# Two slots, one product and one dependency moved in the mixer of a two-layer decoder trunk

## The chip, the cores and the metric

The kernel runs on one core of a Trainium2 chip. The core has engines that run side by side, each with its own list of instructions in a fixed order: PE (TensorE) multiplies matrices and transposes, PEld is its loading of weights, DVE (VectorE) and ACT (ScalarE) do elementwise work, POOL (GpSimd) a few small operations, and SP issues the DMA transfers. The metric is the time of one execution in microseconds (us) on the device; smaller is better. Times of single instructions come from one profiled execution.

## The reference

The input x is 256 tokens by 1024 channels in float32. Two layers follow each other, each with a SwiGLU feed-forward (FFN 1), a mixer and a second SwiGLU feed-forward (FFN 2), all three with a residual and a layer norm:

```python
for l in range(DEPTH):
    x = layer_norm(ALPHA * x + 0.5 * swiglu(x, ffn1_gate[l], ffn1_up[l], ffn1_down[l]), ln_g[l, 0], ln_b[l, 0])
    h = x @ w_in[l]
    ...
    y_pool = multiscale_pool(u, pool_w[l], pool_scale[l])
    o = hgrn2_recurrence(q.astype(f32), f_raw.astype(f32), v.astype(f32), lb_all[l])
    y_hgrn = head_rms_norm(o, hgrn_norm_g[l]) * jax.nn.silu(g.astype(f32))
    mix = jnp.concatenate([y_pool.astype(x.dtype), y_hgrn.astype(x.dtype)], axis=-1) @ w_out[l]
    x = layer_norm(ALPHA * x + mix, ln_g[l, 1], ln_b[l, 1])
    x = layer_norm(ALPHA * x + 0.5 * swiglu(x, ffn2_gate[l], ffn2_up[l], ffn2_down[l]), ln_g[l, 2], ln_b[l, 2])
```

The recurrence has four heads of 128 channels. Per head it is causal linear attention with a decay per channel: with b the running sum of log f, the score of query t on key s is the sum over d of q[t,d] k[s,d] exp(b[t,d] - b[s,d]) for s up to t, k = (1 - lb) sigmoid(-f_raw), and the output is scores times v. The matrices x @ W are 1024 wide on the contracted side; the hidden width of the FFN is 2816.

## The kernel before, in words

The 256 tokens are two halves (`hf` 0 and 1) of 128 partitions. Every float32 product of a weight matrix is three matmuls on rounded operands: high by high, high by low, low by high (`mm3`, L96 to L98). The high part is a cast on ACT (L102), the low part the difference on DVE (L103); names with `h` and `l` at the end are such pairs (`wh`, `wl` for the weights of the gates and projections, `dh`, `dl` for the down projection, `xt` for x transposed, `hth`, `htl` for the hidden values). A weight comes as a tile of 512 KB into one of five `raw` buffers; it is cast and split, which frees the raw buffer for the next load.

The FFN takes its hidden width in 11 groups. For the first two groups, `G` (L300 and L96 to L98) makes gate and up for a half into one PSUM tile, `gate` applies the silu on ACT (L333) and the product `hn` on DVE (L334), `T` transposes hn on PE (L406), and `D` is the down projection into `acc`. After the last group comes `layer_norm`: a residual sum (L243), statistics (L244, L245), the root on POOL, then two operations per half row on DVE (L250, L251). The normed x is transposed in two parts of four 128x128 transposes each (L177).

The mixer projects onto five blocks: f, q, v, g and u. From f it makes the key `kn` by a chain of DVE and ACT operations (`post_f`, tiles tA, tB, tC); `flip` (L574) transposes kn and the query, four transposes each, into kT and qT. `decays` builds exponentials EA and EB for a head (L634 on PE, L635 on ACT), multiplies them with kT and qT on DVE (L640, L652) and, for one strip, copies on POOL (L664). `grams` computes the scores of a pair of heads with small matmuls (L681, L686) and selects them into `Pm` under masks (L698, L700). `diagonal` writes the score of a token with itself into Pm. `cross` makes the scores between the halves, `output` the products with v (L722).

What sets the order: PE's list is written by hand, in the order in which the Python code issues it. A counter of slots advances by one with each `mm3`, three 128x512 matmuls; `later(n, f)` runs `f` n slots on, so that small pieces of work fall between the matmuls of a projection. Functions queued for the same slot run in the order in which they were queued. The lists of the other engines are set when the program is built, by priorities and by when a result is expected; `high_priority` (gates, hidden values) moves work ahead and a negative offset (loads, casts and splits of weights) moves it back. Each engine then takes its list strictly in order and waits at an instruction whose operand is not there.

The parts that the change touches:

Of the kernel before, what the change touches and what calls it, by code (L numbers as in the profile page):

```python
# [14 lines left out]
ALU = mybir.AluOpType  # L15
PSUM = bass.MemoryType.PSUM

P = 128
# [56 lines left out]
def trunk(ctx: ExitStack, tc: tile.TileContext, t, out: bass.AP):  # L75
# [153 lines left out]
    def load_gb(l, i):  # L229
# [3 lines left out]
        late_dma(b, t["ln_b"][l, i:i + 1, :].to_broadcast([P, D]))  # L233
        return g, b

    def layer_norm(hf, accs, scale, gb, slots, last=False):
        z = xp.tile([P, D], F32, name="x")
        st = sp.tile([P, 2, 6], F32, name="st")
        mv = sp.tile([P, 2], F32, name="mv")
        rs = sp.tile([P, 1], F32, name="rs")  # L240
        for c in range(2):
            cs = slice(c * 512, c * 512 + 512)
            nc.vector.scalar_tensor_tensor(z[:, cs], accs[c], scale, x[hf][:, cs], ALU.mult, ALU.add)  # L243
            nc.vector.bn_stats(st[:, c, :], z[:, cs])  # L244
        nc.vector.bn_aggr(mv, st.rearrange("p a b -> p (a b)"))  # L245
        nc.vector.tensor_scalar_add(rs, mv[:, 1:2], LN_EPS / ALPHA ** 2)
        nc.gpsimd.tensor_tensor(rs, rs, neghalf[:, 0:1], ALU.pow)
        for c in range(2):
            cs = slice(c * 512, c * 512 + 512)
            nc.vector.scalar_tensor_tensor(z[:, cs], z[:, cs], mv[:, 0:1], gb[0][:, cs], ALU.subtract, ALU.mult)  # L250
            nc.vector.scalar_tensor_tensor(z[:, cs], z[:, cs], rs, gb[1][:, cs], ALU.mult, ALU.add)  # L251
            if last:
                nc.sync.dma_start(out[hf * P:(hf + 1) * P, cs], z[:, cs])
        x[hf] = z
        pinned[0] = PINNED
        if not last:
            xT[hf] = Transposed(hf, z, slots)


    class FFN:  # L260
        def __init__(self, l, w, ln_i, first=False, last=False):
            gu, dn = t["gu"][l, w], t["dn"][l, w]
            self.first, self.last, self.mixer_next = first, last, not w
            self.slots = ((16, 18), (16, 18) if w else (13, 14))
            self.accs = [None, None]
            self.gw, self.dw, self.ht = {}, {}, {}
            self.ln = (l, ln_i)
            self.gb = None
            for g in range(NG):
                self.gw[g] = []  # L270
                for kq in range(4):
                    extra = (4 * g + kq) % (NW + NX) >= NW
                    self.gw[g].append(Weight(gu[g, kq], *(("x", NX) if extra else ("w", NW)), first and g == 0))
                for n in {0: [], 1: [0, 1], 2: [], NG - 1: [NG - 2, NG - 1]}.get(g, [g - 1]):
                    self.dw[n] = [Weight(dn[2 * n + i], "d", ND) for i in range(2)]
# [53 lines left out]
        def gate(self, g, hf, ps):  # L329
            sil = scope[0].tile([P, GW], F32, name="sil", bufs=2)  # L330
            hn = scope[0].tile([P, GW], F32, name="hn", bufs=2)
            with tc.high_priority(offset=AHEAD):
                nc.scalar.activation(sil, ps[:, 0:GW], AF.Silu)  # L333
                nc.vector.tensor_tensor(hn, sil, ps[:, GW:2 * GW], ALU.mult)  # L334

            slots = {(NG - 1, 0): 2, (NG - 1, 1): 4, (1, 1): 4}
            later(slots.get((g, hf), 6), lambda: self.T(g, hf, hn))

        def start(self):
# [179 lines left out]
    def mixer(l, win, wout):  # L519
# [22 lines left out]
        def post_f(hf, ps):  # L542
            f = mp.tile([P, 512], F32, name="tA", bufs=2)
            nc.scalar.copy(f, ps)
            tmp = mp.tile([P, 512], F32, name="tB", bufs=2)
            ls = mp.tile([P, 512], F32, name="tC", bufs=2)
            log_sigmoid(ls, f, tmp)
            if l > 0:
                nc.vector.tensor_tensor(ls, ls, lm, ALU.add)
            kn[hf] = mp.tile([P, 512], F32, name="kn")  # L550
            nc.vector.tensor_tensor(f, ls, f, ALU.subtract)
            nc.scalar.activation(kn[hf], f, AF.Exp)
            if l > 0:
                nc.vector.tensor_tensor(tmp, ls, la, ALU.subtract)
                nc.vector.tensor_tensor(ls, ls, la, ALU.max)
                nc.scalar.activation(tmp, tmp, AF.Abs)
                nc.scalar.activation(tmp, tmp, AF.Exp, scale=-1.0)
                nc.scalar.activation(tmp, tmp, AF.Ln, bias=1.0)
                nc.vector.tensor_tensor(ls, ls, tmp, ALU.add)

            lf[hf] = [mp.tile([P, 512], F32R, name=n, bufs=2) for n in ("la", "lb")]
            first, second = slice(0, 64), slice(64, P)
            for part, here, there in zip(lf[hf], (first, second), (second, first)):
                nc.scalar.copy(part[here], ls[here])
                nc.vector.tensor_tensor(part[there], ls[here], part[here].bitcast(F32), ALU.subtract)

            def go():
                kT[hf] = flip(kn[hf], "kT")
            later(13, go)

        def flip(nat, name):
            pt = psg.tile([P, NH * P], F32, name="gu").rearrange("p (k t) -> p k t", k=NH)
# [6 lines left out]
        def post_q(hf, ps):  # L579
            A256[hf] = mp.tile([P, NH, P], F32, name=f"A{hf}")  # L580
            q = mp.tile([P, 512], F32, name="tA", bufs=2)
            nc.scalar.activation(q, ps, AF.Copy, scale=float(P) ** -0.5)
            def go():
                qT[hf] = flip(q, "qT")
                later(5, lambda: diagonal(hf, q))
                lag = 7 + 4 * l
                for h in range(NH):
                    later(lag + 2 * h, lambda h=h: decays(hf, h))
                later(lag + 9, lambda: grams(hf, 0))
                later(lag + 14, lambda: grams(hf, 1))  # L590
                if hf == 1:
                    later(lag + 17, cross)
            later(4, go)

        def diagonal(hf, q):
# [3 lines left out]
            nc.vector.tensor_tensor(flat, q, kn[hf], ALU.mult)  # L599
            nc.vector.tensor_reduce(dg, prod, mybir.AxisListType.X, ALU.add)  # L600
            Pm[hf] = mp.tile([P, NH, P], F32, name="Pm", bufs=2)
            for h in range(NH):
                nc.vector.tensor_scalar_mul(Pm[hf][:, h, :], ident, dg[:, h:h + 1])

# [17 lines left out]
        def decays(hf, h):  # L624
# [19 lines left out]
            both = halved(EA[:, :, 0:512])  # L644

            side = (k, q)[hf]
            near, other = (1, 0) if hf == 0 else (0, 1)
            ts = [slice(0, 64), slice(64, P)]
            mul(far[:, :, ts[near]], both[:, :, near, fars:fars + 64], side[:, :, ts[near]])
            whole = c1[:, :, top + 63:top + 64] if hf == 0 else c0[:, :, fars + 63:fars + 64]  # L650
            for i in range(2):
                nc.vector.scalar_tensor_tensor(far[:, i, ts[other]], both[:, i, other, fars:fars + 64], whole[:, i, :],  # L652
                                               side[:, i, ts[other]], ALU.mult, ALU.mult)

            mul(halved(EA[:, :, 512:640]), both[:, :, :, top + 128:top + 192], halved(k))
            low, up = halved(k)[:, :, :, 0:32], halved(q)[:, :, :, 32:64]
# [146 lines left out]
        for hf in range(2):  # L803
# [12 lines left out]
                wout[kt].used()  # L816
            if hf == 0:
                place.reverse()
            layer_norm(hf, accs, 1.0 / ALPHA, gb, (15, 17) if hf else (13, 15))
        return guard  # L820

    phases = []
# [85 lines left out]
```

## Time and profile before

| what | us |
|---|---|
| median of 3 runs | 958.29 (958.11 to 958.52) |
| the profiled execution | 958.23 |
| its span, first to last instruction | 956.5 |
| PE busy / DVE busy / ACT busy | 946.6 / 654.8 / 519.6 |
| granted PE clock, share of full speed | 1.0 |

The span is the time from the first to the last instruction of the profiled execution; 1.7 us lie around it. Busy shares are averages over all stages. The timelines below give start and length in us from the span's start; where a row has a bracket, it is the idle time of the engine ahead of it and the instruction that ended it. The next instruction of an engine can start before the last one has ended, so the distance of two starts is what an instruction costs the engine in a dense stretch.

### The profile page before, as it was taken

How to read it: one execution, taken by the hardware profiler on the slowest of the kernel's cores; microseconds unless marked ns; L12 is line 12 of the kernel's file. 1: busy time of each engine (PE TensorE's matmuls, PEld its weight loads, DVE VectorE, ACT ScalarE, POOL GpSimd, SP SyncE). 2: the span in 40 equal slices, each digit the busy share in tenths (PEclk: the TensorE clock that was granted, in tenths of full speed). 3: DMA queues.
4: the chain of work that ended last, by engine and by line, in shares of the span. 5: the costliest groups of instructions: out<-in, count | busy, mean ns of one | idle time of the engine just before them, and what ended most of it. 6: DMA issues, size and time to landing. Idle time of an engine off the chain costs nothing. (4 is left out here: it accounts for less than half of the span.)

```text
span 956.5 us, 13129 instructions
## 1 busy us (share of the span) xinstructions
PE 946.6 (99%) x4817; PEld 800.0 (84%) x4817; DVE 654.8 (68%) x1104; ACT 519.6 (54%) x809; POOL 32.4 (3%) x50
## 2 busy tenths in 40 slices
PE   9999999999999999999999999999999999999996
PEld 7888888888887888888888888888888888888885
DVE  6875656679789765656676565557898896575625
ACT  6765454368456755444445645433985466546420
POOL 0000000001110000000000000000021000000000
PEclk9999999999999999999999999999999999999999
DMA  8977775332627876565346766552327377676301
GB/s 318 336 243 251 254 247 169 109 103 97 219 88 247 311 232 222 191 205 169 123 157 239 237 211 211 174 155 99 110 67 265 112 266 262 222 240 215 114 1 45
DMA packets 50801, 180.22 MB, mean 188 GB/s; under 512 B 6192, under 2 KB 6192, under 8 KB 50736
## 3 DMA queue, kind: packets, MB, share of 16 engines
q1 hardware_dynamic: 50544, 178.85, 55.5%
q8 instruction: 38, 0.62, 0.3%
q0 software_dynamic: 192, 0.53, 0.2%
q14 instruction: 27, 0.22, 0.1%
HBM read 178.30 MB, written 1.05 MB: 188 GB/s over the span
## 5 line engine op out<-in xcount | busy, mean ns | idle before, releaser
L102 ACT CAST wh<-raw 128x1024 fp32r<-128x1024 f32 x196 | 205.1, 1051 | 100.9 <-DMA raw<-in_gu 35.7
L103 DVE TENSOR_TENSOR wl<-raw,wh 128x1024 fp32r<-128x1024 f32 x196 | 235.9, 1219 | 27.0 <-PE gu L300 15.3
L300 PE MATMUL gu<-xt,wh 128*128 128x512 f32 x768 | 180.6, 391 | 0.0
L103 DVE TENSOR_TENSOR dl<-raw,dh 128x1024 fp32r<-128x1024 f32 x88 | 106.5, 1223 | 101.6 <-ACT dh L102 96.0
L300 PEld LDWEIGHTS gu<-xt,wh 128*128 128x128 f32 x768 | 144.1, 188 | 31.7
L102 ACT CAST dh<-raw 128x1024 fp32r<-128x1024 f32 x88 | 91.6, 1049 | 109.7 <-DMA raw<-in_dn 101.3
L96 PE MATMUL acc<-dh,hth 128*128 128x512 f32 x352 | 140.0, 398 | 0.1
L98 PE MATMUL acc<-dh,htl 128*128 128x512 f32 x352 | 138.1, 392 | 0.0
L97 PE MATMUL acc<-dl,hth 128*128 128x512 f32 x352 | 137.4, 390 | 0.0
L96 PE MATMUL gu<-wh,xt 128*128 128x512 f32 x320 | 128.7, 402 | 0.0
L98 PE MATMUL gu<-wh,xt 128*128 128x512 f32 x320 | 125.5, 392 | 0.0
L97 PE MATMUL gu<-wl,xt 128*128 128x512 f32 x320 | 125.0, 391 | 0.0
L300 PE MATMUL gu<-xt,wl 128*128 128x256 f32 x768 | 99.6, 282 | 0.0
L300 PEld LDWEIGHTS gu<-xt,wl 128*128 128x128 f32 x768 | 96.8, 191 | 1.9
L323 DVE TENSOR_TENSOR sil<-gu,sil 128x256 f32<-128x256 f32 x64 | 27.0, 422 | 83.7 <-ACT sil L322 83.7
L98 PEld LDWEIGHTS acc<-dh,htl 128*128 128x128 f32 x352 | 66.0, 188 | 14.8 <-DVE htl L103 0.2
L97 PEld LDWEIGHTS acc<-dl,hth 128*128 128x128 f32 x352 | 66.2, 188 | 12.7 <-DVE dl L103 0.3
L96 PEld LDWEIGHTS acc<-dh,hth 128*128 128x128 f32 x352 | 66.2, 188 | 12.5 <-ACT hth L102 0.5
L98 PEld LDWEIGHTS gu<-wh,xt 128*128 128x128 f32 x320 | 60.1, 188 | 13.1
L97 PEld LDWEIGHTS gu<-wl,xt 128*128 128x128 f32 x320 | 60.2, 188 | 11.4
L96 PEld LDWEIGHTS gu<-wh,xt 128*128 128x128 f32 x320 | 60.1, 188 | 11.0
L300 PE MATMUL gu<-xt,xh 128*128 128x512 f32 x256 | 62.4, 396 | 0.0
(182 smaller groups left out, 1056.2 us busy)
## 6 DMA issues: line engine op xcount, KB each, us to landing
raw<-in_gu SPq DMA_DIRECT2D x172, 512.0 KB, 4.4
raw<-in_dn SPq DMA_DIRECT2D x88, 512.0 KB, 4.6
raw<-in_win SPq DMA_DIRECT2D x40, 512.0 KB, 4.2
raw<-in_wout SPq DMA_DIRECT2D x16, 512.0 KB, 4.2
lng<-in_ln_g SPq DMA_DIRECT2D x6, 512.0 KB, 4.7
lnb<-in_ln_b SPq DMA_DIRECT2D x6, 512.0 KB, 6.0
raw<-in_first SPq DMA_DIRECT2D x5, 384.0 KB, 5.7
x<-in_first SPq DMA_DIRECT2D x3, 384.0 KB, 7.2
```

What stands on the lines that cost most here:

```text
L96: nc.tensor.matmul(ps, lh, wh, start=start, stop=False)
L97: nc.tensor.matmul(ps, lh, wl, start=False, stop=False)
L98: nc.tensor.matmul(ps, ll, wh, start=False, stop=stop)
L102: first = nc.scalar.copy(dst_h, src)
L103: return first, nc.vector.tensor_tensor(dst_l, src, dst_h.bitcast(F32), ALU.subtract)
L300: nc.tensor.matmul(ps[i][part][:, 2 * S - w:], weight.parts[lo][:, c:c + P], x[:, 0:w], start=kt == 0 and not lo, stop=kt == KT - 1 and lo ...
L323: nc.vector.tensor_tensor(dst, p[:, 0:S], dst, ALU.add)
```

## The change

`layer_norm` remembers its last addition. The product hn of the first group and first half, in every FFN but the first, may only be scheduled behind it. The two parts of x's transposes, which had slots of their own, share the earlier slot; in the first FFN the transposes of hn for group 1 of both halves come at slot 5. In the mixer the flip of kn comes at slot 12 after `post_f` in place of 13, the first scores at `lag + 10` in place of 9, and the cross product at `lag + 14`, right behind the second scores of the second half. The diagonal is one product of two broadcast operands in place of four operations. The "far" products, three operations per head pair before, are two: one over the whole tile and one more over a half of it.

```diff
+    normed = [None]
...
-            nc.vector.scalar_tensor_tensor(z[:, cs], z[:, cs], rs, gb[1][:, cs], ALU.mult, ALU.add)
+            normed[0] = nc.vector.scalar_tensor_tensor(z[:, cs], z[:, cs], rs, gb[1][:, cs], ALU.mult, ALU.add)
...
-            self.slots = ((16, 18), (16, 18) if w else (13, 14))
+            self.slots = ((16, 16), (16, 16) if w else (13, 13))
...
-                nc.vector.tensor_tensor(hn, sil, ps[:, GW:2 * GW], ALU.mult)
-
-            slots = {(NG - 1, 0): 2, (NG - 1, 1): 4, (1, 1): 4}
+                mul = nc.vector.tensor_tensor(hn, sil, ps[:, GW:2 * GW], ALU.mult)
+            if (g, hf) == (0, 0) and not self.first:
+
+                tc.add_manual_dep(mul.ins, normed[0].ins.name,
+                                  mybir.DependencyInfo(mybir.DependencyClass.NoSync, mybir.DependencyReason.DATA),
+                                  reason="behind the layer norm")
+
+            slots = {(NG - 1, 0): 2, (NG - 1, 1): 4}
+            slots.update({(1, 0): 5, (1, 1): 5} if self.first else {(1, 1): 4})
...
-            later(13, go)
+            later(12, go)
...
-                later(lag + 9, lambda: grams(hf, 0))
+                later(lag + 10, lambda: grams(hf, 0))
                 later(lag + 14, lambda: grams(hf, 1))
                 if hf == 1:
-                    later(lag + 17, cross)
+                    later(lag + 14, cross)
...
-            for h in range(NH):
-                nc.vector.tensor_scalar_mul(Pm[hf][:, h, :], ident, dg[:, h:h + 1])
+            shape = [P, NH, P]
+            nc.vector.tensor_tensor(Pm[hf], ident.unsqueeze(1).to_broadcast(shape), dg.unsqueeze(2).to_broadcast(shape),
+                                    ALU.mult)
...
-            near, other = (1, 0) if hf == 0 else (0, 1)
-            ts = [slice(0, 64), slice(64, P)]
-            mul(far[:, :, ts[near]], both[:, :, near, fars:fars + 64], side[:, :, ts[near]])
+            ts = slice(64 * hf, 64 * hf + 64)
+            mul(halved(far), both[:, :, :, fars:fars + 64], halved(side))
             whole = c1[:, :, top + 63:top + 64] if hf == 0 else c0[:, :, fars + 63:fars + 64]
-            for i in range(2):
-                nc.vector.scalar_tensor_tensor(far[:, i, ts[other]], both[:, i, other, fars:fars + 64], whole[:, i, :],
-                                               side[:, i, ts[other]], ALU.mult, ALU.mult)
+            mul(far[:, :, ts], far[:, :, ts], whole.to_broadcast([P, 2, 64]))
...
-            layer_norm(hf, accs, 1.0 / ALPHA, gb, (15, 17) if hf else (13, 15))
+            layer_norm(hf, accs, 1.0 / ALPHA, gb, (15, 15) if hf else (13, 13))
```

The lists show what that moves. From L239 on, a line of the changed kernel has a number two to nine higher than before. On PE, at the first scores of layer 0, before (`EA`, `EB`: exponentials; `tA`: the query of the second half; `kn`: its key; the numbers behind names are of buffers):

```order
L98 MATMUL gu_2191<-wh_2033,xt_86 128x512
L681 MATMUL acc_2228<-EA_2111 128x128 x2
L686 MATMUL acc_2229<-EB_2112,EA_2111 128x192 x2
L686 MATMUL acc_2230<-EB_2112,EA_2111 128x256 x2
L574 MATMUL gu_2247<-ident_88,tA_2189 128x128 x4
L96 MATMUL gu_2191<-wh_2052,xt_86 128x512
L97 MATMUL gu_2191<-wl_2053,xt_86 128x512
L98 MATMUL gu_2191<-wh_2052,xt_86 128x512
L574 MATMUL gu_2257<-ident_88,kn_2077 128x128 x4
```

And the same place after:

```order
L98 MATMUL gu_2187<-wh_2040,xt_86 128x512
L582 MATMUL gu_2223<-ident_88,kn_2077 128x128 x4
L582 MATMUL gu_2230<-ident_88,tA_2185 128x128 x4
L96 MATMUL gu_2187<-wh_2052,xt_86 128x512
L97 MATMUL gu_2187<-wl_2053,xt_86 128x512
L98 MATMUL gu_2187<-wh_2052,xt_86 128x512
L687 MATMUL acc_2240<-EA_2108 128x128 x2
L692 MATMUL acc_2241<-EB_2109,EA_2108 128x192 x2
L692 MATMUL acc_2242<-EB_2109,EA_2108 128x256 x2
```

Both flips and a slot now stand ahead of the scores, and kn's flip ahead of the query's. In layer 1 the flips of the second half are at the same distance from each other and in the same new order.

On DVE, at the start of the second FFN of layer 0, before (`x_2969`: the row being normed; `wl`: the splits of the second group's four weights; `hn`: the gate product):

```order
L103 TENSOR_TENSOR wl_2891<-raw_2889,wh_2890 128x1024
L244 BN_STATS st_2970<-x_2969 128x6
L103 TENSOR_TENSOR wl_2910<-raw_2908,wh_2909 128x1024
L245 BN_AGGR mv_2971<-st_2970 128x2
L103 TENSOR_TENSOR wl_2929<-raw_2927,wh_2928 128x1024
L334 TENSOR_TENSOR hn_3010<-sil_3009,gu_2984 128x256
L246 TENSOR_SCALAR rs_2972<-mv_2971 128x1
L250 SCALAR_TENSOR_TENSOR x_2969<-x_2969,mv_2971,lng_2703 128x512 x2
L251 SCALAR_TENSOR_TENSOR x_2969<-x_2969,rs_2972,lnb_2704 128x512 x2
L103 TENSOR_TENSOR dl_2935<-raw_2933,dh_2934 128x1024
```

And after:

```order
L247 BN_AGGR mv_2961<-st_2960 128x2
L103 TENSOR_TENSOR wl_2881<-raw_2879,wh_2880 128x1024
L248 TENSOR_SCALAR rs_2962<-mv_2961 128x1
L252 SCALAR_TENSOR_TENSOR x_2959<-x_2959,mv_2961,lng_2693 128x512 x2
L253 SCALAR_TENSOR_TENSOR x_2959<-x_2959,rs_2962,lnb_2694 128x512 x2
L336 TENSOR_TENSOR hn_3000<-sil_2999,gu_2974 128x256
L103 TENSOR_TENSOR wl_2907<-raw_2905,wh_2906 128x1024
L103 TENSOR_TENSOR wl_2919<-raw_2917,wh_2918 128x1024
L103 TENSOR_TENSOR dl_2925<-raw_2923,dh_2924 128x1024
```

The third and the fourth split of the weights (before 2910 and 2929, after 2907 and 2919) have moved from ahead of hn and the norm's last operations to behind them.

On DVE, in the mixer of layer 1 while the key of the second half is made, before (`tC`, `tA`, `tB`: the steps of that chain; tA, written at L551, is what ACT turns into kn; `Pm` with `ident`: the diagonal of the first half):

```order
L103 TENSOR_TENSOR wl_6507<-raw_6505,wh_6506 128x1024
L603 TENSOR_SCALAR Pm_6497<-ident_88,dg_6494 128x128
L508 SCALAR_TENSOR_TENSOR tC_6468<-tA_6465,tB_6467 128x512
L603 TENSOR_SCALAR Pm_6497<-ident_88,dg_6494 128x128
L549 TENSOR_TENSOR tC_6468<-tC_6468,lm_102 128x512
L603 TENSOR_SCALAR Pm_6497<-ident_88,dg_6494 128x128
L551 TENSOR_TENSOR tA_6465<-tC_6468,tA_6465 128x512
L554 TENSOR_TENSOR tB_6467<-tC_6468,la_101 128x512
L603 TENSOR_SCALAR Pm_6497<-ident_88,dg_6494 128x128
```

And after:

```order
L103 TENSOR_TENSOR wl_6494<-raw_6492,wh_6493 128x1024
L611 TENSOR_TENSOR Pm_6487<-ident_88,dg_6484 128x512
L516 SCALAR_TENSOR_TENSOR tC_6458<-tA_6455,tB_6457 128x512
L103 TENSOR_TENSOR wl_6506<-raw_6504,wh_6505 128x1024
L557 TENSOR_TENSOR tC_6458<-tC_6458,lm_102 128x512
L103 TENSOR_TENSOR wl_6518<-raw_6516,wh_6517 128x1024
L559 TENSOR_TENSOR tA_6455<-tC_6458,tA_6455 128x512
L562 TENSOR_TENSOR tB_6457<-tC_6458,la_101 128x512
```

Two splits of weights, which stood far behind this place before, are now between the steps that make tA.

## Rows read from the trace of the kernel before

**Rows 1.** The page's busy time of each engine, share of the span and instructions.

```profile
PE 946.6 (99%) x4817; PEld 800.0 (84%) x4817; DVE 654.8 (68%) x1104; ACT 519.6 (54%) x809; POOL 32.4 (3%) x50
```

**Rows 2.** Timeline of PE's weight loads at the first scores of layer 0: start, length, instruction, idle time ahead of it and what ended it.

```profile
219.33 0.52 PEld L681 LDWEIGHTS acc<-EA 128*128 128x128 f32 x4 [0.54 <-ACT EA L635]
220.28 0.62 PEld L686 LDWEIGHTS acc<-EB,EA 128*128 128x128 f32 x4 [0.42 <-issue]
221.17 0.73 PEld L686 LDWEIGHTS acc<-EB,EA 128*128 128x128 f32 x4 [0.27 <-POOL EB L664]
```

**Rows 3.** Timeline of PE's matmuls there: the last projection matmul ahead of the scores, the flip of the query behind them, and a stretch of the flip of kn cut at three transposes.

```profile
218.83 0.39 PE L98 MATMUL gu<-wh,xt 128*128 128x512 f32 x1
...
222.14 0.60 PE L574 MATMUL gu<-ident,tA 128*128 128x128 f32 x4
...
223.27 0.49 PE L574 MATMUL gu<-ident,kn 128*128 128x128 f32 x3
```

**Rows 4.** Timelines of DVE, POOL and ACT there: the last products of EA with the query, the products for EB, POOL's copy, and ACT's copy of the second half's query.

```profile
218.73 0.49 DVE L640 TENSOR_TENSOR EA<-EA,qT 128x128 f32<-128x128 f32 x2
...
219.74 1.03 DVE L640 TENSOR_TENSOR EB<-EB,qT 128x128 f32<-128x128 f32 x5
...
219.98 1.13 POOL L664 COPY EB<-qT 128x128 f32<-128x128 f32 x1 [26.09 <-DVE EA L640]
...
217.81 0.60 ACT L582 ACTIVATE tA<-gu 128x512 f32<-128x512 f32 x1
```

**Rows 5.** Timeline of DVE in the mixer of layer 1, while the key of the second half is made.

```profile
686.36 1.22 DVE L103 TENSOR_TENSOR wl<-raw,wh 128x1024 fp32r<-128x1024 f32 x1
687.49 0.28 DVE L603 TENSOR_SCALAR Pm<-ident,dg 128x128 f32<-128x128 f32 x1
687.77 0.69 DVE L508 SCALAR_TENSOR_TENSOR tC<-tA,tB 128x512 f32<-128x512 f32 x1
688.38 0.29 DVE L603 TENSOR_SCALAR Pm<-ident,dg 128x128 f32<-128x128 f32 x1
688.58 0.69 DVE L549 TENSOR_TENSOR tC<-tC,lm 128x512 f32<-128x512 f32 x1
689.18 0.29 DVE L603 TENSOR_SCALAR Pm<-ident,dg 128x128 f32<-128x128 f32 x1
```

**Rows 6.** Timeline of DVE at the start of the second FFN of layer 0: the fourth weight split, hn, and the norm.

```profile
296.79 1.17 DVE L103 TENSOR_TENSOR wl<-raw,wh 128x1024 fp32r<-128x1024 f32 x1
298.05 0.42 DVE L334 TENSOR_TENSOR hn<-sil,gu 128x256 f32<-128x256 f32 x1
298.38 0.15 DVE L246 TENSOR_SCALAR rs<-mv 128x1 f32<-128x1 f32 x1
298.45 1.40 DVE L250 SCALAR_TENSOR_TENSOR x<-x,mv,lng 128x512 f32<-128x512 f32 x2
299.77 1.41 DVE L251 SCALAR_TENSOR_TENSOR x<-x,rs,lnb 128x512 f32<-128x512 f32 x2
```

**Rows 7.** Timeline of PE there: the first matmul on the third split, the end of the second group, the first down matmuls; and, last, the first matmul on the third split in layer 1.

```profile
299.58 0.39 PE L97 MATMUL gu<-wl,xt 128*128 128x512 f32 x1
...
302.54 0.40 PE L98 MATMUL gu<-wh,xt 128*128 128x512 f32 x1
303.03 0.50 PE L96 MATMUL acc<-dh,hth 128*128 128x512 f32 x1
303.37 0.39 PE L97 MATMUL acc<-dl,hth 128*128 128x512 f32 x1
...
304.18 0.48 PE L96 MATMUL acc<-dh,hth 128*128 128x512 f32 x1
304.62 0.50 PE L97 MATMUL acc<-dl,hth 128*128 128x512 f32 x1
...
771.88 0.39 PE L97 MATMUL gu<-wl,xt 128*128 128x512 f32 x1
```

**Rows 8.** Timeline of ACT there: the cast that waited for its load, and the cast of the hidden values behind it.

```profile
301.66 1.05 ACT L102 CAST dh<-raw 128x1024 fp32r<-128x1024 f32 x1 [1.14 <-DMA raw<-in_dn]
302.61 0.37 ACT L102 CAST hth<-gu 128x256 fp32r<-128x256 f32 x1
```

**Rows 9.** Timeline of PE in the mixer of layer 1: the flips of the second half.

```profile
691.72 0.60 PE L574 MATMUL gu<-ident,tA 128*128 128x128 f32 x4
...
693.33 0.60 PE L574 MATMUL gu<-ident,kn 128*128 128x128 f32 x4
```

**Rows 10.** Timeline of ACT there: an exponential of the decays and that of the key.

```profile
690.02 0.62 ACT L635 ACTIVATE EA<-acc 128x512 f32<-128x512 f32 x1
690.49 0.67 ACT L552 ACTIVATE kn<-tA 128x512 f32<-128x512 f32 x1
```

**Rows 11.** Waits over the whole span, who for whom: us in total, times, longest.

```profile
PEld acc L686 <- issue: 0.7, 2, 0.4
...
ACT dh L102 <- DMA raw<-in_dn: 101.3, 58, 5.2
```

**Rows 12.** Timeline of PE in the second FFN of layer 1, at a transpose of hn.

```profile
792.24 0.39 PE L98 MATMUL acc<-dh,htl 128*128 128x512 f32 x1
792.78 0.44 PE L406 MATMUL gu<-ident,hn 128*128 128x128 f32 x2 [0.15 <-DVE hn L334]
```

**Rows 13.** The page's DMA issues: queue, operation and count, size of one, and median us from issue to landing.

```profile
raw<-in_dn SPq DMA_DIRECT2D x88, 512.0 KB, 4.6
```

## The prediction

> **What bounds the kernel now.** I read the page's busy times first, then the waits, then PE's timeline around each wait, and beside it DVE's and ACT's. The page shows PE busy 99% of the span against 68% for DVE and 54% for ACT [rows 1]. So an instruction less on DVE is worth nothing by itself: the time falls only where PE waits for a result, and rises only where a result comes later than PE asks. I therefore list PE's waits near the edits, see which go, and then look for new ones. The program is scheduled when it is built, each engine takes its list in order, and the lists of the changed kernel are known; the times I lay on them are the trace's.
>
> The profiled execution took 958.23 us (span 956.5 and 1.7 around it); the median of the runs is 958.29, so the sum is made against 958.23 and the answer moved up by 0.06. A change of 0.2% is 1.9 us.
>
> **Scores a slot later, flips of k and q together (layer 0).** At the first scores PE's weight loads stand idle 0.54, 0.42 and 0.27 us, released by the exponentials and by POOL's copy [rows 2]: 1.2 us. On PE the last projection matmul starts at 218.83, the flip behind the scores at 222.14 [rows 3]. In the new order both flips come at 219.06 (218.83 and a 0.23 step), then three matmuls, then the scores. A transpose costs 0.11 (four take 0.60, three 0.49 [rows 3]), so eight take 0.8, and the slot with its first, slower matmul 0.8: the scores start at 220.65. The products for EA end at 219.22, those for EB at 220.77, POOL's copy at 221.12 [rows 4]; the loads that take the copy follow the first by 1.15 (219.33 to 221.17 less the two waits [rows 2]), at 221.8. All is there even if DVE gains nothing. The flips find their sources ready: q's copy ended at 218.41 [rows 4], and kn stands ahead of it in ACT's list. Gain **1.2**, between 0.9 (part of a load's idle time is there in any group) and 1.3.
>
> **Diagonal in one operation, far products whole.** Four TENSOR_SCALAR steps of 0.20 (688.38 to 688.58 [rows 5]) become one TENSOR_TENSOR of 128x512 with two broadcast operands. The trace has no such operand. The nearest row, 128x512 with plain operands, steps 0.60 (688.58 to 689.18 [rows 5]); the other end is the four pieces, 0.80. I take 0.60. The far products give back some 0.1 per head pair. DVE has no PE waiting there, so the gain is 0; the cost is one of position: the four pieces stood between the steps of the next gate, and now the whole stands ahead.
>
> **The layer norm ahead of the second FFN.** The new dependency puts the gate product hn behind the whole norm, and both transposes of x come at one slot, so the build also moves DVE's third and fourth weight splits behind hn. Before, the third was done when the fourth started, at 296.79 [rows 6]. Now the scalar step (0.07), two subtractions (1.32), two additions (1.33) and hn (0.33), each by the distance to the next start [rows 6], come before it ends: 296.79 + 3.05 = 299.84, and 0.09 for the end behind the last step, 299.93. PE wants that split at 299.58 [rows 7]; with 0.05 of signalling a **new wait of 0.40**. The fourth ends 1.13 later and is wanted 1.4 later. Layer 1 has the same rows (its matmul at 771.88 [rows 7]): **0.40** again. Each is bounded by 0.2, if the earlier transposes let the norm begin sooner, and 0.6.
>
> In layer 0 PE also waits at the first down projection: steps 302.54 to 303.03 (0.49 for 0.23), 303.03 to 303.37 (0.34 for 0.23) and 304.18 to 304.62 (0.44 for the 0.31 behind transposes) [rows 7]: 0.26 + 0.11 + 0.13 = 0.50. The first is hth, which on ACT stood behind a cast of dh that started only at 301.66 [rows 8]. In the new list that cast stands behind hth, and the splits dl are ready by 303.7. Gain **0.50** (0.3 to 0.7). Next late there is the gate of the second group, priced as a rival.
>
> **The k flip of layer 1.** This is the largest loss. PE's second-half flips stood at 691.72 (q) and 693.33 (kn) [rows 9]; now kn's is first, at 691.72. DVE's list has the diagonal and two splits of 1.13 (686.36 to 687.49 [rows 5]) in the chain that makes kn. From 687.49: diagonal 0.60, tC 0.61, split 1.13, tC 0.60, split 1.13, tA 0.69 to its end: 692.25. The casts of both splits stand ahead of the last exponential of that chain in ACT's list, so DVE finds them done. ACT's list has the exponential kn behind one EB, one cast and one EA more: 690.49 + 0.47 + 0.95 + 0.47 = 692.4 (steps from [rows 8, 10]). With its own 0.67 [rows 10] kn is there at 693.07, and PE waits **1.4**. The lower end is 1.2 (ACT free at once); the upper 1.7 (diagonal 0.80 and slower signalling). PE is then 1.4 later, which covers DVE's later work of this layer: the wait of 0.27 at a score matmul (0.7 in two waits, less 0.42 [rows 2, 11]) goes, **+0.27** (0 to 0.27).
>
> A word on those steps: a 0.69 us operation has its successor start after 0.60 [rows 5]. By the Trainium skill, VectorE: DVE Perf Modes, "The DRAIN you can't avoid", the next operation does not start until the pipe is empty. By that rule each step would cost its full duration, some 0.09 more: 0.3 more at the k flip and 0.5 at each norm, and the sum would come out 1.3 worse. The trace does not agree for these independent neighbours, 0.60 against 0.69, and the measured step decides.
>
> **Small ones.** The wait for hn at 792.78 (0.54 behind 792.24, for 0.23 [rows 12]) stood behind a split on DVE; PE comes 0.4 later there: **+0.31** (0 to 0.31). Fifteen pairs of four transposes that now share a slot save one 0.11 in place of 0.03 each less what the next matmul loses, about 0.01 a pair: **+0.15** (0 to 0.3). The cross product behind the scores and T of the first FFN only change places among work whose sources are ready: 0.
>
> **The sum.** 1.20 + 0.50 - 0.40 - 0.40 - 1.40 + 0.27 + 0.31 + 0.15 = +0.23 us gained: 958.0 for the profile, 958.06 against the median. I give 958.0, no change that a measurement can tell.
>
> **Rivals.**
> - *The k flip is not late.* If PE finds kn in time, the 1.4 stays in hand: 958.29 - 1.63 = 956.7. For it: over the span DVE is idle a third of the time and ACT nearly half [rows 1]. Against: DVE shows no gap in these rows [rows 5], and the lists are in order. Even this is 0.17%; with the high ends of the other gains it passes 0.2%.
> - *Slower: late buffers behind the norm.* The late third split also frees its raw buffer late, at 299.93 in place of 296.8 [rows 6]. A load takes 4.6 us to land [rows 13], so the fourth dh cast starts at 304.5, and the new ACT list has the second group's silu behind it: silu by 305.9, hn by 306.2. PE wants hn's PSUM buffer after the twelve down matmuls, at 302.54 + 0.23 + 0.40 + 0.45 (second transposes) + 12 x 0.228 = 306.35. It decides from a landing of 4.8 us on. The waits for dh are up to 5.2 us long [rows 11], so a landing of 6 is possible: 1.2 in each layer, 2.4 in all, 958.06 + 2.4 = 960.5. At 5.2 us it is 0.4 each: 958.9. Against: the usual landing still leaves 0.15 us.
> - *Steps cost their full length.* Where the new lists set dependent operations side by side, a step may cost 0.69 and not 0.60: 0.5 at each norm and 0.3 at the k flip, 958.06 + 1.3 = 959.4. Against: the norm's operations read each other's results and two of them still step by 1.32 [rows 6].
> - *The gains stay out.* The scores' wait only moves to the next scores (DVE's list of the second pair is not shorter): 958.06 + 1.2 = 959.3.
>
> **How the numbers follow.** Forecast 0.63, with its own range 957.4 to 958.8; full-length steps 0.03; k flip in time 0.14; late buffers 0.12, of which two thirds beyond 960.2; gains stay out 0.08. Faster by over 0.2% (under 956.4) takes half of the first rival and a little of the forecast: 0.10. Slower (over 960.2) 0.09. The rest, 0.81, is within 0.2%, which is about what a measurement of this kernel can tell. The range reaches from 956.4 (first rival) to 959.6 (gains stay out, the milder late buffers).
>
> **What the profile will show.** Right: no wait at layer 0's first scores; DVE's third split of the second FFN ending 0.4 behind its matmul, in both layers; a gap of 1.2 to 1.7 us on PE ahead of the kn flip of layer 1, released by ACT's exponential. Wrong: no such gap at that flip (then nearer 956.7), or PE waiting for hn's PSUM buffer behind the first down projection (then nearer 960).

## The result and the profile after

The changed kernel takes 959.89 us (median of 21 runs, 959.13 to 960.51), the kernel before 958.29 in the same number of runs beside it. The ratio is 1.0014, with a 95% interval of 1.0008 to 1.0020: slower by some 1.3 us, 0.8 to 1.9 (the ratio goes by means; the medians lie 1.6 apart). The forecast was 958.0 with a range up to 959.6, so the time lies above the range, and it moved the other way than the sum said. The profiled execution took 959.71 us with a span of 957.7, 1.2 us more than before.

PE is as busy as before, and DVE has no more to do. The page's busy times after, answering to [rows 1]:

```profile
PE 946.1 (99%) x4817; PEld 800.9 (84%) x4817; DVE 652.9 (68%) x1084; ACT 516.9 (54%) x808; POOL 36.5 (4%) x50
```

PEld has 0.9 us more; the one engine with clearly more to show is POOL, 36.5 us in place of 32.4, with the same 50 instructions. The waits of the weight loads over the whole span say who that hurts; columns are who waited for whom, us in total, times, longest:

```profile
PEld acc L692 <- POOL EB L670: 1.6, 2, 0.9
PEld gu L582 <- ACT kn L560: 1.5, 1, 1.5
PEld gu L97 <- DVE wl L103: 1.3, 2, 0.6
```

The second and the third were forecast. The first is at the score matmuls, where the forecast had no wait left. To see what each place cost I set the start of the same projection or down matmul in the two traces side by side. It is the second or third matmul behind each place: the first is slower behind transposes than behind other matmuls, and its neighbours are not the same in the two lists.

| behind | before | after | after minus before |
|---|---|---|---|
| the first down matmul of the program | 28.31 | 27.98 | -0.33 |
| flips of layer 0, first half | 207.06 | 206.71 | -0.35 |
| first scores of layer 0 | 223.94 | 223.10 | -0.84 |
| first down matmuls of layer 0's second FFN | 304.96 | 303.92 | -1.04 |
| flips of layer 1, first half | 680.22 | 679.27 | -0.95 |
| flips of layer 1, second half | 693.99 | 694.29 | +0.30 |
| scores of layer 1, first half | 703.45 | 704.17 | +0.72 |
| scores of layer 1, second half | 724.46 | 725.70 | +1.24 |
| start of layer 1's second FFN | 776.70 | 778.34 | +1.64 |
| first hn of its third stretch | 793.29 | 794.55 | +1.26 |

The change is ahead by 0.84 us after layer 0's first scores and loses 2.2 in layer 1. The first row is the start of the program, which no edit touches: in the traces of the experiments this matmul lies between 0.73 us earlier and 0.24 later than before. It is left out of each comparison of traces below.

**The first scores of layer 0.** Timeline of PE after, answering to [rows 3]:

```profile
218.43 0.39 PE L98 MATMUL gu<-wh,xt 128*128 128x512 f32 x1
218.66 0.60 PE L582 MATMUL gu<-ident,kn 128*128 128x128 f32 x4
...
220.22 0.60 PE L687 MATMUL acc<-EA 128*128 128x128 f32 x4
220.67 0.82 PE L692 MATMUL acc<-EB,EA 128*128 128x192 f32 x4
221.90 1.13 PE L692 MATMUL acc<-EB,EA 128*128 128x256 f32 x4 [0.42 <-POOL EB L670]
```

The scores start 1.56 us behind the first flip, as forecast (220.65 less 219.06 is 1.59), and the first of them find their operands. The last four stand: 1.23 us from the start of the group ahead to their own, where an unhindered group ahead of it has 0.65 (four steps of 0.16). Timelines of POOL and DVE there, answering to [rows 4]:

```profile
218.95 2.90 POOL L670 COPY EB<-qT 128x128 f32<-128x128 f32 x1 [24.83 <-DVE EA L649]
...
218.38 0.42 DVE L649 TENSOR_TENSOR EA<-EB,kT 128x256 f32<-128x256 f32 x1
218.71 1.30 DVE L649 TENSOR_TENSOR EB<-EB,qT 128x192 f32<-128x192 f32 x6
219.93 0.42 DVE L649 TENSOR_TENSOR A<-EA,kT 128x256 f32<-128x256 f32 x1
220.27 0.42 DVE L649 TENSOR_TENSOR EA<-EA,kT 128x256 f32<-128x256 f32 x1
220.60 0.28 DVE L649 TENSOR_TENSOR A<-A,EA 128x128 f32<-128x128 f32 x1
220.81 0.49 DVE L649 TENSOR_TENSOR EA<-EA,kT 128x128 f32<-128x128 f32 x2
221.21 0.49 DVE L649 TENSOR_TENSOR EA<-EA,qT 128x128 f32<-128x128 f32 x2
221.61 0.52 DVE L649 TENSOR_TENSOR EA<-EB,kT 128x256 f32<-128x256 f32 x1
222.06 1.40 DVE L649 TENSOR_TENSOR EB<-EB,qT 128x192 f32<-128x192 f32 x6
```

POOL's copy starts 1.0 us earlier than before and ends 0.74 later: it is 2.90 us long, and was 1.13. All that time DVE runs products of two tensors, each starting before the last has ended. The copy ends at 221.85, beside the first product that is longer than its kind: that of 221.61 lasts 0.52 in place of 0.42, and the next starts 0.45 behind it in place of 0.33. Whether DVE paused there and let the copy in, or the copy held the product, the trace does not tell.

**The scores of layer 1, second half.** The same at its worst; timelines of POOL, DVE and PE:

```profile
711.44 4.47 POOL L670 COPY EB<-qT 128x128 f32<-128x128 f32 x1 [10.22 <-DVE EA L649]
...
714.46 1.29 DVE L649 TENSOR_TENSOR EB<-EB,qT 128x192 f32<-128x192 f32 x6
715.67 0.36 DVE L704 COPY_PREDICATED Pm<-masks,acc 128x192 f32<-128x192 uint8 x1
...
714.55 0.82 PE L692 MATMUL acc<-EB,EA 128*128 128x192 f32 x4
715.97 1.13 PE L692 MATMUL acc<-EB,EA 128*128 128x256 f32 x4 [0.60 <-POOL EB L670]
```

The copy waits through two head pairs of products and ends at 715.91, inside DVE's next COPY_PREDICATED. PE stood about 0.77 us (714.55 to 715.97 is 1.42, against 0.65 where nothing is waited for).

**The scores of layer 1, first half.** Here PE stands too, and not for POOL (PE after, then the weight loads' wait in the run x1 below, which has no copy on POOL):

```profile
702.01 0.82 PE L692 MATMUL acc<-EB,EA 128*128 128x192 f32 x4
703.00 1.10 PE L692 MATMUL acc<-EB,EA 128*128 128x256 f32 x4 [0.17 <-DVE Pm L704]
...
PEld acc L692 <- ACT Pm L696: 0.4, 1, 0.4
```

702.01 to 703.00 is 0.99, against 0.65: 0.34 for the copies of the scores into Pm, on DVE or ACT. In the table this place costs 0.42 (+0.30 to +0.72).

**The flip of kn.** PE, DVE and ACT there, answering to [rows 5, 9, 10]:

```profile
690.50 0.40 PE L98 MATMUL gu<-wh,xt 128*128 128x512 f32 x1
691.96 0.66 PE L582 MATMUL gu<-ident,kn 128*128 128x128 f32 x4 [1.05 <-ACT kn L560]
...
686.48 0.69 DVE L611 TENSOR_TENSOR Pm<-ident,dg 128x512 f32<-128x512 f32 x1
687.08 0.68 DVE L516 SCALAR_TENSOR_TENSOR tC<-tA,tB 128x512 f32<-128x512 f32 x1
687.68 1.22 DVE L103 TENSOR_TENSOR wl<-raw,wh 128x1024 fp32r<-128x1024 f32 x1
688.82 0.68 DVE L557 TENSOR_TENSOR tC<-tC,lm 128x512 f32<-128x512 f32 x1
689.42 1.22 DVE L103 TENSOR_TENSOR wl<-raw,wh 128x1024 fp32r<-128x1024 f32 x1
690.55 0.68 DVE L559 TENSOR_TENSOR tA<-tC,tA 128x512 f32<-128x512 f32 x1
...
690.72 0.63 ACT L644 ACTIVATE EA<-acc 128x512 f32<-128x512 f32 x1
691.27 0.63 ACT L560 ACTIVATE kn<-tA 128x512 f32<-128x512 f32 x1
```

690.50 to 691.96 is 1.46 for a step of 0.23: a wait of 1.23. The diagonal with broadcast operands steps 0.60 (686.48 to 687.08), and tA ends 4.75 us behind the start of the diagonal; the forecast had 4.76.

**The second FFN of layer 0.** DVE and PE, answering to [rows 6, 7]:

```profile
296.08 1.41 DVE L253 SCALAR_TENSOR_TENSOR x<-x,rs,lnb 128x512 f32<-128x512 f32 x2
297.40 0.42 DVE L336 TENSOR_TENSOR hn<-sil,gu 128x256 f32<-128x256 f32 x1
297.73 2.36 DVE L103 TENSOR_TENSOR wl<-raw,wh 128x1024 fp32r<-128x1024 f32 x2
...
298.41 0.39 PE L96 MATMUL gu<-wh,xt 128*128 128x512 f32 x1
299.01 0.50 PE L97 MATMUL gu<-wl,xt 128*128 128x512 f32 x1 [0.21 <-DVE wl L103]
299.35 0.39 PE L98 MATMUL gu<-wh,xt 128*128 128x512 f32 x1
```

298.41 to 299.01 is 0.60 for 0.23, and the matmul behind it comes 0.11 late as well: 0.48.

### The profile page after: what moved, and what is told of

Same layout as the page of the kernel before. It is cut to its first block, busy times and chain, and to the rows that moved or that the text cites. A ratio compares the mean times of both kernels' runs of the same rounds, so it can differ in the third digit from the quotient of the medians.

```text
span 957.7 us, 13108 instructions
## 1 busy us (share of the span) xinstructions
PE 946.1 (99%) x4817; PEld 800.9 (84%) x4817; DVE 652.9 (68%) x1084; ACT 516.9 (54%) x808; POOL 36.5 (4%) x50
```

## The experiments

My theory from the two traces: POOL's copy can make no headway while DVE runs products of two tensors one behind the other; the new far products took the SCALAR_TENSOR_TENSOR out of that run, so the copy ends 1 to 3 us later, and PE's last score matmuls with it. Rivals: the scores come before DVE itself is done, and POOL is only last in the row; or the loss is the two forecast waits (flip of kn, third split) alone, and POOL's share is chance. The kernel before ran beside every group of runs, with medians of 958.51 (x1 to x4), 958.06 (x5 to x8) and 958.70 (x9 to x12).

**x1, the copy on DVE.**

```diff
-            nc.gpsimd.tensor_copy(EB[:, :, S32:S32 + 32], q[:, :, 1::2])
+            nc.vector.tensor_copy(EB[:, :, S32:S32 + 32], q[:, :, 1::2])
```

> The changed kernel with POOL's copy of every other query column into EB made on DVE instead (8 operations of some 0.2 us more there). Theory (POOL's copy stands still while DVE runs products of two operands without a gap, 2.9 us at the first scores of layer 0): the three waits of PE at the score matmuls (about 0.7, 0.4 and 0.9 us) go, and the time falls by 1.5 to 2.0 us against the changed kernel, to about 958.2. Rival (the scores come before DVE's products are done, POOL is only the last in the row): DVE is 0.2 later, the waits stay at 0.3 us or more each, and the time falls by less than 0.8.

958.40 us, ratio to before 0.9998 (0.9989 to 1.0007). 1.5 us less than the changed kernel. The two waits for POOL at the scores are gone: the two traces part by 0.67 us at the first scores of layer 0, by some 0.8 at the last of layer 1, and by no more than 0.2 at any other place behind the start. That is the theory's number. The third wait that I had listed, 0.4, stayed, so it was not POOL's.

**x2, the far products as before.**

```diff
...
-            mul(halved(far), both[:, :, :, fars:fars + 64], halved(side))
...
-            mul(far[:, :, ts], far[:, :, ts], whole.to_broadcast([P, 2, 64]))
+            mul(far[:, :, ts[near]], both[:, :, near, fars:fars + 64], side[:, :, ts[near]])
...
+                nc.vector.scalar_tensor_tensor(far[:, i, ts[other]], both[:, i, other, fars:fars + 64], whole[:, i, :],
+                                               side[:, i, ts[other]], ALU.mult, ALU.mult)
```

> The changed kernel with the far products in their old form (one product and two SCALAR_TENSOR_TENSOR per head pair). Theory a (it is the SCALAR_TENSOR_TENSOR that let POOL in, between two head pairs): POOL's first copy of layer 0 shrinks from 2.9 to about 1.2 to 1.5 us, the wait at the first scores goes, 0.7 us or more come back. Theory b (any dense run on DVE keeps POOL out, whatever its form): the copy stays above 2 us and the time within 0.3 us of the changed kernel.

958.57 us, ratio 0.9999 (0.9990 to 1.0008). The eight copies are 0.97 to 1.57 us long; timelines of POOL and DVE at the first scores of layer 0:

```profile
218.92 1.14 POOL L673 COPY EB<-qT 128x128 f32<-128x128 f32 x1 [25.18 <-DVE EA L649]
...
219.82 0.52 DVE L661 SCALAR_TENSOR_TENSOR A<-EA,kT 128x64 f32<-128x64 f32 x2
```

The copy starts where it did in the changed kernel (218.95 there) and ends at 220.06, within the first SCALAR_TENSOR_TENSOR. Theory a. 1.3 us came back. In the trace the wait at the flip of kn is shorter as well (0.5 us on PE in place of 1.1), and a new wait of 0.7 us for the copy of the cross product came up elsewhere; so this run moves more than the copy, and it is x1 that prices it.

**x3, the flip of kn at slot 13 again.**

```diff
-            later(12, go)
+            later(13, go)
```

> The changed kernel with the flip of kn at slot 13 again. Theory (kn comes late in layer 1 because two weight splits and the diagonal stand ahead of it on DVE): the wait of 1.2 us ahead of that flip goes, and 0.8 to 1.3 us of the time. Rival (that wait only covered others): PE is then earlier at layer 1's scores, POOL's copies are as late as ever, and the waits there grow by 0.5 us or more; the time falls by less than 0.6.

960.14 us, ratio 1.0013 (1.0004 to 1.0022): nothing came back. In the trace PE gains 1.25 us at the flip of layer 1 and loses it at the scores, some 0.5 at layer 0's first, which come earlier now and meet the same late copy, and 0.6 at layer 1's; the waits for POOL in the weight loads are:

```profile
PEld acc L692 <- POOL EB L670: 2.7, 3, 1.1
```

2.7 us in place of 1.6. The rival held: with POOL late, the slot and the wait ahead of the flip had only paid for a part of the waits at the scores.

**x4, the transposes of x at slots of their own again.**

```diff
-            self.slots = ((16, 16), (16, 16) if w else (13, 13))
+            self.slots = ((16, 18), (16, 18) if w else (13, 14))
...
-            layer_norm(hf, accs, 1.0 / ALPHA, gb, (15, 15) if hf else (13, 13))
+            layer_norm(hf, accs, 1.0 / ALPHA, gb, (15, 17) if hf else (13, 15))
```

> The changed kernel with the two parts of x's transposes at slots of their own, as before. Theory (sharing a slot is what put two weight splits behind the layer norm): the waits of 0.5 us for the third split in both second FFNs go; in layer 0 some 0.3 of the wait for hth may return; the time falls by 0.6 to 1.0 us. Rival (the new dependency of hn on the norm is what does it): the waits of 0.5 us stay, the time is within 0.3 us.

962.60 us, ratio 1.0039 (1.0027 to 1.0052). Both were wrong. The wait for the third split did go (the slots had put it behind the norm), but PE now waits for gate products further on, where splits stand ahead of them on DVE:

```profile
PEld gu L414 <- DVE hn L336: 4.9, 5, 1.7
```

in place of 0.8. The slots and the dependency are one design: with the dependency kept, the old slots leave hn late.

**x5, the far products alone, in the kernel before.** The new two lines of the change's far products, nothing else.

> The kernel before with the new far products alone. Theory (they take away the SCALAR_TENSOR_TENSOR between two head pairs, and with them the place where POOL's copy gets on): POOL's copies of EB grow, at least three of the eight beyond 2 us where one was, the waits of PE for that copy grow from 0.3 to 1.0 us or more, and the time rises by 0.5 to 1.5 us, to about 959.3. Rival (the change's other parts are needed for it, the scores a slot later above all): the copies stay near 1.1 us, the time within 0.3 us of before.

964.27 us (961.4 to 966.2), ratio 1.0057 (1.0041 to 1.0072): 6.2 us more than before, four times the upper end of what I had expected. The waits of PE's weight loads, and the longest copy (4.47 us, in one row with a short one behind it):

```profile
PEld acc L683 <- POOL EB L661: 4.2, 2, 2.5
PEld gu L406 <- DVE hn L334: 2.4, 2, 1.6
...
715.78 4.71 POOL L661 COPY EB<-qT 128x128 f32<-128x128 f32 x2 [11.91 <-DVE EA L640]
```

Two of the eight copies are beyond 2 us (2.63 and 4.47), not three as the theory had it, one takes 1.27, and five take 0.37 or less; but the two long ones are those PE wants soon. Alone, the edit is far worse than in the changed kernel, where the profile has PE waiting 1.0 us for POOL in place of 3.6; that the later scores and earlier flips hide the rest there was not tried apart.

**x6, two spare operations.** In the changed kernel, per head pair, two operations into a tile that nothing reads:

```diff
+            near, other = (1, 0) if hf == 0 else (0, 1)
+            spare = mp.tile([P, 2, 64], F32, name="spare")
+            for i in range(2):
+                nc.vector.scalar_tensor_tensor(spare[:, i, :], both[:, i, other, fars:fars + 64], whole[:, i, :],
+                                               side[:, i, 64 * other:64 * other + 64], ALU.mult, ALU.mult)
```

> The changed kernel with two SCALAR_TENSOR_TENSOR of 128x64 per head pair added on DVE, into a tile that nothing reads, at the place where the old far products had theirs. Theory: although DVE has 0.4 us more to do per head pair, POOL's first copies end sooner: the first of layer 0 in 1.0 to 1.5 us in place of 2.9, the wait of PE there goes. Rival (it is DVE's total work, or the new products themselves): the copy stays at 2.5 us or more, and the scores wait longer than in the changed kernel.

957.66 us in its one execution, 2.2 less than the changed kernel's median (the lowest of its 21 runs is 959.13), with sixteen more operations on DVE. In the trace 0.7 and 0.9 us of that are at the two scores that waited for POOL, and 0.5 is at the flip of kn, which waits less here, as in x2. POOL and DVE at the first scores of layer 0:

```profile
219.92 1.29 POOL L675 COPY EB<-qT 128x128 f32<-128x128 f32 x1 [25.50 <-DVE EA L649]
...
220.63 0.42 DVE L649 TENSOR_TENSOR A<-EA,kT 128x256 f32<-128x256 f32 x1
220.96 0.33 DVE L663 SCALAR_TENSOR_TENSOR spare<-EA,kT 128x64 f32<-128x64 f32 x1
221.22 0.28 DVE L649 TENSOR_TENSOR A<-A,EA 128x128 f32<-128x128 f32 x1
```

The copy ends at 221.21, within the first spare operation, which lasts 0.33 (the second, with no copy beside it, 0.27). For the copy's length this is the plainest of the runs: in the source work was only added, and the copy became shorter.

**x10, the same with an operation that reads one tensor.** `nc.vector.tensor_scalar_mul(spare[:, i, :], side[:, i, 0:64], whole[:, i, :])` in place of the two.

> As the run with the two spare SCALAR_TENSOR_TENSOR, but with two TENSOR_SCALAR of 128x64, which read one tensor and a scalar per partition. Theory a (any operation that reads one tensor lets POOL in): the first copy of layer 0 is 1.0 to 1.5 us long as there. Theory b (it is the form SCALAR_TENSOR_TENSOR that leaves a gap): the copy stays at 2.5 us or more.

958.62 us in one execution; the eight copies are 0.98 to 1.57 us long, the first 1.28, so theory a. Both forms that let POOL in carry a scalar per partition, and the SCALAR_TENSOR_TENSOR reads two tensors beside it: so the number of tensors alone isn't what decides, and which property does was not tried apart. The time is 1.0 above x6, and the trace has the wait of 0.7 for the cross product that x2 showed as well; but single executions of one kernel lie that far apart too (957.34 to 960.76 for the kernel before).

**x11, the far products alone with the copy on DVE.**

> The kernel before with the new far products and the copy on DVE. With the far products alone PE waited 3.6 us for POOL's copy; those waits go. Theory (that wait is the cost, and the rest of the 6 us there is what a later DVE adds at the second FFN): 3 to 4.5 us of the 6 come back, the time is 959.5 to 961. Rival (the list that the build makes around the new products costs by itself, copy or not): less than 2 us come back.

959.19 us, ratio 1.0005 (0.9996 to 1.0014): 0.5 above the kernel before beside it, where x5 was 6.2 above. That is 5 us or more back, more than expected, since the waits for hn and for x at the second FFN went with the wait for POOL. PE still waits 1.3 us at one score matmul, now for DVE's masks.

**x12, the kernel before with the copy on DVE.**

> The kernel before with the copy on DVE alone. PE waits 0.3 us for POOL's copy there, so by the theory no more than 0.1 to 0.4 us can come of it: 957.7 to 958.2. Rival (moving the copy is a gain of its own, of the 1.5 us it brought to the changed kernel): 957.0 or less.

958.16 us, ratio 0.9997 (0.9988 to 1.0006): as the theory says, there was little to win there. So moving the copy is no gain of 1.5 us by itself, and x1's gain takes back a loss that the change had made.

**x7, x8 and x9, on top of x1.** x7 puts the flip of kn back to slot 13; x8 also puts the slots of x back and takes the dependency out (`if False:`); x9 is x7 with the mixer's x at slots 15 and 16, and 13 and 14.

> The changed kernel with the copy on DVE and the flip of kn at slot 13. Theory (undoing the flip alone gained nothing because POOL's copies took the time back): now the 1.2 us ahead of that flip are really gone, the time falls by 0.8 to 1.3 us against the copy on DVE alone, to about 957.3. Rival (whatever stands behind that flip in layer 1 waits for DVE anyway): within 0.4 us of the copy on DVE alone, 958.0 or more.

957.54 us, ratio 0.9993 (0.9984 to 1.0001). The median is 0.9 below x1, but the kernel before was 0.45 lower beside it too, and the two intervals overlap: by the times it is not shown to be a gain. In the trace 1.2 us are gained at the flip, and 0.6 lost again at 705, where a PSUM buffer waits for DVE's masks: half the theory, half the rival.

> The same, and the slots of x's transposes and the order of hn and the norm as before. Theory (the slots and the dependency belong together: either alone costs, both undone give the start of the second FFN back as it was): the two waits of 0.5 us for the third split go, the wait for hth in layer 0 (0.5 to 0.7) comes back, no long wait for hn; the time within 0.5 us of the kernel with copy and flip alone. Rival (the old slots cost by themselves): the time rises by 1 us or more, as with the slots alone undone.

957.73 us, ratio 0.9995 (0.9986 to 1.0004), no different from x7: slots and dependency undone together cost nothing and gain nothing that the times show. The wait for hth in layer 0 that I had expected back did not come: PE's weight loads wait 0.2 us there, for dl.

> The changed kernel with copy on DVE, kn's flip at slot 13, and the two transposes of the mixer's x one slot apart in place of together; the build then puts the third split of the second FFN ahead of the norm's last operations again, the fourth behind hn. Theory (that split's place is what PE waits for there): both waits of 0.5 us go and nothing comes for them, the time falls by 0.7 to 1.1 us against copy and flip alone, to about 956.6, below both kernels. Rival (the fourth split or hn is late next, as with the slots of before): a wait of 0.3 us or more at each place, the time within 0.4 us.

957.15 us, ratio 0.9986 (0.9978 to 0.9995). The waits for the third split are gone, 0.46 us each in the trace, and given back to others, in the weight loads' waits:

```profile
PEld gu L414 <- DVE hn L336: 1.2, 1, 1.2
...
PEld acc L97 <- DVE dl L103: 1.0, 2, 0.6
```

That is the rival. Against x7 it is no gain that the runs show (0.4 us between medians, intervals that overlap, and in its trace the program's start was 0.6 earlier and the rest 0.3 slower). Against the kernel before it is the only version whose interval lies clear on the faster side, 0.5 to 2.1 us, and it is 2.7 us below the changed kernel; one of ten intervals is thin evidence for so small a gain.

## Why the prediction was wrong, step by step

**The step that failed** is in "Scores a slot later": "POOL's copy at 221.12", and "All is there even if DVE gains nothing". I took the copy's end from the trace of before, 1.13 us long [rows 4], as if its length were its own. It is not: before, that copy ended beside the SCALAR_TENSOR_TENSOR of the next head pair (timeline of DVE before), which the change removes, and I had counted that removal as "the gain is 0".

```profile
220.88 0.52 DVE L652 SCALAR_TENSOR_TENSOR A<-EA,kT 128x64 f32<-128x64 f32 x2
```

After, the copy is 2.90 us long, ends at 221.85, and the gain at that place is 0.49 in place of 1.20. x2, x6 and x10 move the copy's length by DVE's forms (2.9 to 1.1, 1.3 and 1.3 us). x1 takes the copy away, and its trace gains 1.17 at that place: with the copy out of the way the forecast's 1.20 was right.

**The same mistake in the k flip's last sentence**: "PE is then 1.4 later, which covers DVE's later work of this layer". It did not cover POOL's copy at the second half: 0.52 lost there (+0.72 to +1.24 in the table) in place of 0.27 gained, a miss of 0.79. In x1, without POOL's copy, this place does gain 0.27. Nor did it cover all of DVE's and ACT's work: 0.42 went at the first half's scores, a wait that the sum did not have and that x1 has too. POOL's two misses are 1.5 of the 1.7 us between the forecast and the profiled execution (1.9 to the median); the 0.42 and the smaller terms of both signs make up the rest.

**What was right.** The k flip: 1.23 us for 1.40, DVE's chain to within 0.01 and the diagonal at its plain step of 0.60; ACT's steps were 0.1 shorter than taken. The third split: 0.48 for 0.40 in each layer; the 0.08 is the matmul behind it, which comes 0.11 late and which I left out. The first down matmuls: the waits went, and 0.58 came for 0.50. The wait for hn in layer 1 went; 0.38 for 0.31. The pairs of transposes: nothing visible, as good as forecast. The start of the program gave 0.33 in this execution, which belongs to no edit.

**The rule on the steps.** The rule weighed in the prediction, that each step costs its full length, did not hold here either: L611 lasts 0.69 and its successor starts after 0.60. The Trainium skill, VectorE: DVE Perf Modes, "The DRAIN you can't avoid", itself adds that "a next op that is not held starts earlier", which the prediction left out.

**The rivals.** The k flip was late, so the first fell. The late buffers did not come: no wait for a PSUM buffer behind the first down projection. The last, "the scores' wait only moves to the next scores", is the nearest in kind to what happened: PE waited at the scores. But its reason was another, DVE's list and not POOL, and that its price, 1.2, comes near the 1.35 us that PE stood for POOL is luck. It was given 0.08.

**What I had missed.** The Trainium skill, GPSIMD Engine Reference, "Specifications", says that GpSimd's interfaces to SBUF are shared with VectorE, with contention beside DVE instructions that have two SBUF inputs. The trace of before already had the sign: the same copy of 128x128 lasted between 0.30 and 2.38 us. The runs agree as to products of two tensors (2.90 and 4.47 us), though some copies got through beside them at once (0.30 us). With SCALAR_TENSOR_TENSOR, two tensors and a scalar, they don't fit it as plainly: the copy ends beside it.

## What to carry to other kernels

Where the same small operation of POOL has lengths far apart in one trace, its length may belong to what DVE runs beside it, as here: look up which DVE instruction each of them ends at, before a change removes that instruction. Fewer and larger products on DVE can cost time when PE waits for POOL; moving POOL's few columns to DVE, 0.2 us each, was worth 1.5 us here. And a new wait on the critical engine can hide others behind it, so undoing it alone (x3) may show nothing: take away the wait behind it first, and then undo it. In x7's trace 1.2 us came that way and 0.6 stayed; the times are too close to confirm it.

## What the runs showed of the hardware that was not expected

- A copy of 128x128 on POOL took 0.30 to 4.47 us. Where it did not get through at once, it lasted until DVE's run of TENSOR_TENSOR ended or until one product was 0.10 longer than its kind; otherwise it ended beside COPY_PREDICATED, SCALAR_TENSOR_TENSOR or TENSOR_SCALAR, or in a gap. An operation that let it in took 0.06 longer itself (0.33 for 0.27 in x6).
- DVE's list does not settle the length alone. Some copies of 0.30 to 0.37 us ended in the middle of a run of products, beside a 128x128 product of 0.39 in place of 0.28: two of the eight before (at 235.47 and 710.76), four in x5. The same copy in the same place of DVE's list, in x3 and in the changed kernel:

```profile
700.81 0.30 POOL L670 COPY EB<-qT 128x128 f32<-128x128 f32 x1 [2.68 <-DVE EA L649]
...
699.98 1.24 POOL L670 COPY EB<-qT 128x128 f32<-128x128 f32 x1 [2.88 <-DVE EA L649]
```

  What decides between the two was not found.
- The long copies repeat: the first of layer 0 was 2.90, 2.88 and 2.88 us in the changed kernel, x3 and x4, whose DVE lists are the same there.
- A TENSOR_TENSOR of 128x512 with both operands broadcast steps 0.60 us, the same as with plain ones.
